# A MoE layer's gate factor in its third matrices, its residual in the experts' sum, and its last norm's sums on ScalarE

## The chip, the cores and the metric

The kernel runs on one core of a Trainium2 chip. The metric is the device time of one execution, in microseconds. The core's engines are TensorE (PE, with its weight loads apart as PEld), VectorE (DVE), ScalarE (ACT), GpSimd (POOL) and SyncE (SP, which here only starts transfers). Each engine runs its own instructions in order, and waits for the others through semaphores.

## What is computed

One decoder layer over 2048 tokens of 1024 features: a token mixer with its norm, then a mixture of experts with 64 routed experts (eight for each token) and one shared expert of 256 hidden features each. The edit touches the second half alone. Cut to that, the reference is:

```python
def layer_norm(x, g, b):
    xf = x.astype(jnp.float32)
    mu = xf.mean(-1, keepdims=True)
    var = jnp.square(xf - mu).mean(-1, keepdims=True)
    return ((xf - mu) * lax.rsqrt(var + LN_EPS)).astype(x.dtype) * g + b

def swiglu(t, w1, w3, w2):
    return (jax.nn.silu(t @ w1) * (t @ w3)) @ w2

x = layer_norm(ALPHA * x + g1 * (mixed @ w_out[l]), ln_mix_g[l], ln_mix_b[l])
h = x * (1 + sc2) + sh2
y = moe_ffn(h, ...)     # sum over a token's 8 experts of gate * swiglu, plus the shared swiglu
x = layer_norm(ALPHA * x + g2 * y, ln_ffn_g[l], ln_ffn_b[l])
```

`g2` is a vector of 1024 factors, one for each output feature, the same for all tokens. The third matrix `w2` of an expert has the output features as its columns.

## The kernel before

The first 2075 us are the mixer, its projection, its norm and the router (`phase_c` writes `ALPHA * x1`, the scaled result of the first norm, to a DRAM tensor `x1` at L1792). Then `moe_phase` (L1953 on) works through a list of units. A unit is up to 320 tokens of one set of weights. First come three units of the shared expert, 256 tokens each (set "s"), then the 64 experts, a large one and a small one in turn, each cut into one to three units, then the other 10 blocks of 128 tokens of the shared expert (set None, with its weights loaded a second time). A token block has 128 tokens.

For each set, `weights` (L1986) loads the three matrices in six halves of 512 KB: SP issues the load into one of four `wraw` buffers (L1994), ScalarE copies it to a rounded matrix (L1998), and VectorE subtracts the two for a second, small matrix (L1999), since each product runs as three matmuls of such parts. Only for the set None is the last matrix multiplied by `g2b`, a copy of `g2` on all partitions, before that (L1997). `hidden` (L2019) makes the first two products (L2051, or L2032 for at most 128 tokens), the silu on ScalarE and the product `s` on VectorE (L2057, L2038), and splits it into `gH` (ScalarE, L61) and `gL` (VectorE, L64). `transposed` does the same for the input (`hH`, `hL`) from PSUM banks named `tr`. `back` (L2060) multiplies `gH` and `gL` with the third matrix into two PSUM banks `py`. A unit's `back` is woven into the `hidden` of the unit that follows.

What happens to `py` depends on the set. `routed` scales it by the token's gate on ScalarE (L2102), and GpSimd adds it with an indirect transfer into rows of the DRAM tensor `acc` (L2103). `begin` (L2302, shared set, first six blocks) copies it on ScalarE (L2306) and writes it to `acc`; other rows of `acc` were set to zero earlier (L1567). `finish` (L2286, other ten blocks) ends the layer. It calls `sums` (L2276), which loads a block of `x1` (L2279) and, behind the last scatter-add, of `acc` (L2281), multiplies `acc` by `g2b` (L2282) and adds the two (L2283); it adds `py` to that (L2297), and starts `norm` (L2257): two statistics (L2262), their aggregate (L2264), the variance plus epsilon (L2266), a reciprocal root in ten small operations on one column (L650 to L655), two products (L2272, L2273) and the store (L2274). The six blocks that `begin` had taken need only `sums` and `norm`; one of them joins each of the first six blocks of `finish`.

The blocks under way take turns (`norms`), and a scheduler places every instruction in its engine's queue by priorities and by its own estimate of times. `y` of `finish` is one of eight buffers cut out of the weight pool (`buffer`).

## Time and profile before

| | us |
| --- | --- |
| median of three runs | 3769.25 (3760.10 to 3776.89) |
| the profiled execution | 3762.49 |
| its span on the core | 3760.8 |
| TensorE busy in the span | 3433.5 (91%) |
| VectorE busy | 2670.9 (71%) |
| ScalarE busy | 1941.9 (52%) |
| GpSimd busy | 883.3 (23%) |

The span is the time from the first to the last instruction of the profiled execution; 1.7 us lie around it. Shares are over the whole span, and hide that the stages have different limits. Times in the trace are counted from the span's start. A row of groups gives the line, the engine, the operation, the tiles written and read with their shapes, the count, the busy time and the mean of one, and the idle time of the engine just before. `<-` in brackets names what ended a wait.

### The profile page before, as it was taken

The page shows a single profiled execution, that of the slowest core. Times are in us where ns is not written, and L with a number is a line of the kernel's source. Part 1 is how long each engine was busy: PE and PEld are TensorE (multiplying, and loading weights), DVE is VectorE, ACT ScalarE, POOL GpSimd, SP SyncE. Part 2 cuts the span into 40 slices and gives each one's busy share as a digit, 9 for nine tenths or more (in the row PEclk, how much of TensorE's full clock was granted, in tenths as well). Part 3 has the DMA queues.
Part 4 walks back from the last instruction along what each step waited for, and adds up shares of the span by engine and source line. Part 5 has one row for each costly group of instructions (what it writes and reads, how often), then busy time and mean ns, then how long its engine had stood idle before and what let it go on. Part 6 is the DMA issues. An engine that isn't in the chain of part 4 may idle for free. (4 is left out here: it accounts for less than half of the span.)

```text
span 3760.8 us, 64004 instructions
## 1 busy us (share of the span) xinstructions
PE 3433.5 (91%) x23044; PEld 2984.6 (79%) x23044; DVE 2670.9 (71%) x7039; ACT 1941.9 (52%) x3439; POOL 883.3 (23%) x817
## 2 busy tenths in 40 slices
PE   7799999799999878999897899999999999999994
PEld 5577777688888767778786799888899888888983
DVE  6556899888888678888799555555665555665669
ACT  4233656355555567766322355555565555556630
POOL 1000000322223255543000122233233223232200
PEclk9899999899999889999998899999999999999997
DMA  7657466400000132222543488888899888888973
GB/s 253 210 192 242 141 216 221 164 27 21 24 24 18 30 107 81 78 69 80 172 149 129 163 213 218 234 237 233 246 266 252 242 223 235 241 248 254 295 226 138
DMA packets 276234, 640.37 MB, mean 170 GB/s; under 512 B 34428, under 2 KB 115364, under 8 KB 275784
## 3 DMA queue, kind: packets, MB, share of 16 engines
q1 hardware_dynamic: 231760, 481.09, 38.1%
q0 software_dynamic: 40832, 150.32, 18.1%
q10 hardware_dynamic: 3320, 4.83, 0.4%
q8 instruction: 182, 2.98, 0.3%
q14 instruction: 140, 1.15, 0.1%
HBM read 467.14 MB, written 169.00 MB: 169 GB/s over the span
## 5 line engine op out<-in xcount | busy, mean ns | idle before, releaser
L2051 PE MATMUL p<-hH,w 128*128 128x256 f32 (+8 forms) x4352 | 872.2, 288 | 9.3 <-DVE w L1999 6.6
L2051 PEld LDWEIGHTS p<-hH,w 128*128 128x128 f32 x4352 | 706.0, 191 | 18.8 <-DVE w L1999 6.9
L1999 DVE TENSOR_TENSOR w<-wraw,w 128x1024 fp32r<-128x1024 f32 x396 | 474.8, 1223 | 285.7 <-ACT w L1998 268.9
L2051 PE MATMUL p<-hL,w 128*128 128x256 f32 (+8 forms) x2176 | 615.9, 283 | 0.7 <-DVE hL L64 0.7
L1998 ACT ACTIVATE w<-wraw 128x1024 fp32r<-128x1024 f32 x396 | 406.1, 1053 | 232.0 <-DMA wraw<-in_exp_w_dram 102.0
L2066 PE MATMUL py<-w,gH 128*128 128x512 f32 (+5 forms) x1384 | 443.8, 403 | 26.2 <-DVE w L2297 14.6
L2103 POOL DMA_INDIRECT scratch_acc<-y,idx x157 | 263.9, 1681 | 797.5 <-ACT y L2102 245.8
L2051 PEld LDWEIGHTS p<-hL,w 128*128 128x128 f32 x2176 | 415.9, 191 | 6.2 <-DVE hL L64 0.9
L285 PE MATMUL pj<-hTH,w 128*128 128x512 f32 x1152 | 379.1, 404 | 21.5 <-ACT w L201 16.4
L64 DVE TENSOR_TENSOR hL<-tr,hH 128x512 fp32r<-128x512 f32 (+7 forms) x346 | 213.0, 626 | 210.9 <-ACT hH L61 192.7
L2066 PEld LDWEIGHTS py<-w,gH 128*128 128x128 f32 (+5 forms) x1384 | 240.5, 182 | 86.7 <-DVE w L2297 15.8
L2102 ACT ACTIVATE y<-py,gt 128x512 f32<-128x512 f32 (+5 forms) x314 | 213.9, 683 | 147.3 <-PE py L2066 131.3
L285 PEld LDWEIGHTS pj<-hTH,w 128*128 128x128 f32 x1152 | 221.9, 194 | 76.0 <-ACT w L201 20.4
L61 ACT ACTIVATE hH<-tr 128x512 fp32r<-128x512 f32 (+7 forms) x346 | 184.0, 544 | 189.6 <-PE tr L2011 165.4
L2066 PE MATMUL py<-w,gL 128*128 128x512 f32 (+5 forms) x692 | 275.9, 399 | 0.3 <-DVE gL L64 0.3
L2077 POOL DMA_INDIRECT x<-scratch_h,idx x157 | 163.5, 1041 | 309.9 <-DVE L L2119 68.5
L285 PE MATMUL pj<-hTL,w 128*128 128x512 f32 x576 | 231.2, 401 | 0.0
L2011 PE MATMUL tr<-ident,x 128*128 128x128 f32 (+5 forms) x1384 | 192.2, 266 | 31.5 <-issue 20.7
L2011 PEld LDWEIGHTS tr<-ident,x 128*128 128x128 f32 (+5 forms) x1384 | 149.8, 141 | 42.7 <-issue 26.0
L2066 PEld LDWEIGHTS py<-w,gL 128*128 128x128 f32 (+5 forms) x692 | 125.2, 181 | 40.0 <-DVE gL L64 1.7
L2032 PE MATMUL p<-w,hH 128*128 128x256 f32 (+2 forms) x736 | 142.6, 291 | 10.7 <-DVE s L2057 10.7
L61 ACT ACTIVATE gH<-s 128x256 fp32r<-128x256 f32 (+8 forms) x136 | 55.1, 405 | 160.4 <-DVE s L2057 147.8
(610 smaller groups left out, 8199.9 us busy)
## 6 DMA issues: line engine op xcount, KB each, us to landing
wraw<-in_exp_w_dram SPq DMA_DIRECT2D x384, 512.0 KB
w<-scratch_wH SPq DMA_DIRECT2D x57, 512.0 KB
w<-scratch_wL SPq DMA_DIRECT2D x57, 512.0 KB
mw<-in_w_mod_dram SPq DMA_DIRECT2D x48, 512.0 KB
scratch_rw<-po SPq DMA_DIRECT2D x44, 256.0 KB
w<-in_w_in_dram SPq DMA_DIRECT2D x21, 512.0 KB
x<-in_x_dram SPq DMA_DIRECT2D x40, 256.0 KB
scratch_wH<-w SPq DMA_DIRECT2D x19, 512.0 KB
```

The source lines that it names most:

```text
L61: nc.scalar.activation(hi, src, AF.Copy)
L64: (lo_eng or nc.vector).tensor_tensor(lo, src, hi.bitcast(F32), op=ALU.subtract)
L285: nc.tensor.matmul(ps, lhsT=a_[:, k, :], rhs=b_[k], start=(k == 0 and i == 0), stop=(k == KT - 1 and i == 2))
L1998: ACT.activation(wh[:, c], raw, AF.Copy)
L1999: V.tensor_tensor(wl[:, c], raw, wh[:, c].bitcast(F32), op=ALU.subtract)
L2011: PE.transpose(ps[:, k * n:(k + 1) * n], x[0:n, (4 * h + k) * P:(4 * h + k + 1) * P], g.ident[0:n, 0:n])
L2032: PE.matmul(ps[i][:n, 0:256], lhsT=(hH, hL)[a][:, k, 0:n], rhs=w[i][b][:, k, :], start=(k == 0 and j == 0), stop=(k == KT - 1 and j == 2))
L2051: PE.matmul(ps[i][:, 0:n], lhsT=w[i][a][:, k, m * P:(m + 1) * P], rhs=(hH, hL)[b][:, k, 0:n], start=(k == 0 and j == 0), stop=(k == KT - 1 ...
L2066: PE.matmul(ps[:n], lhsT=(gH, gL)[a][:, m, c:c + n], rhs=w[2][b][:, m, h * CH:(h + 1) * CH], start=(m == 0 and j == 0), stop=(m == 1 and j ...
L2077: G.indirect_dma_start(out=x[0:m, :], out_offset=None, in_=S["h2"], in_offset=bass.IndirectOffsetOnAxis(ap=ix[0:m], axis=0))
L2102: ACT.activation(y[:m, hs], ps[:m], AF.Copy, scale=gt[:m])
L2103: G.indirect_dma_start(out=S["acc"], out_offset=bass.IndirectOffsetOnAxis(ap=ix[0:m], axis=0), in_=y[0:m, :], in_offset=None, compute_op=A ...
```

## The change

Three edits hang together. `weights` multiplies the third matrix of every set by `g2b`, so `acc` collects sums that are already scaled. `phase_c` writes `ALPHA * x1` into `acc` itself, `begin` loads it, adds the shared expert's part on VectorE and writes it back, and the routed scatter-adds go on top: at the end `acc` holds all of the norm's input but the shared expert's last part. And the norm takes its row sum from the instruction that makes the row (an accumulator output, L2308; for the six blocks of `begin` two copies on ScalarE, L2301), its mean from those (L2264), and its variance from a square on ScalarE with the negative mean as bias and an accumulator output (L2266).

```diff
@@ phase_c
-            nc.sync.dma_start(S["x1"][t0:t0 + P, :], xh)
+            nc.sync.dma_start(S["acc"][t0:t0 + P, :], xh)
@@ weights
-                    if scaled and s is srcs[-1]:
+                    if a == 2:
                         V.tensor_tensor(raw, raw, g2b, op=ALU.mult)
@@ norm
-            for n in range(2):
-                V.bn_stats(out=st[:, n, :], in_=y[:, n * CH:(n + 1) * CH])
-            mv = sm.tile([P, 2], F32, name="lnmv")
-            V.bn_aggr(out=mv, in_=st)
-            va = sm.tile([P, 1], F32, name="lnva")
-            V.tensor_scalar(va, mv[:, 1:2], 1e-5, None, op0=ALU.add)
-            rs = rsqrt(nc, sm, va, [P, 1], None, "ln")
+            for i, (rows, y, su) in enumerate(blocks):
+                V.tensor_scalar(mean[:, i:i + 1], su[:, 0:1], su[:, 1:2], -1.0 / D, op0=ALU.add, op1=ALU.mult)
+                junk = xg.tile([P, HC], F32, name="x")[:, 0:D]
+                ACT.activation(junk, y, AF.Square, bias=mean[:, i:i + 1], accum_out=sq[:, i:i + 1])
+            yield
+            va = sm.tile([P, 2], F32, name="lnva")[:, 0:n]
+            V.tensor_scalar(va, sq, 1.0 / D, 1e-5, op0=ALU.mult, op1=ALU.add)
+            rs = rsqrt(nc, sm, va, [P, n], None, f"ln{n}")
@@ sums
-            nc.sync.dma_start(y, S["x1"][rows, :])
-            a = xg.tile([P, HC], F32, name="x")[:, 0:D]
-            nc.sync.dma_start(a, S["acc"][rows, :])
-            V.tensor_tensor(a, a, g2b, op=ALU.mult)
-            V.tensor_tensor(y, y, a, op=ALU.add)
-            return y
+            nc.sync.dma_start(y, S["acc"][rows, :])
+            return y, sm.tile([P, 2], F32, name="lnsu", bufs=8)
@@ finish
+                    for q in range(2):
+                        hs = slice(q * CH, (q + 1) * CH)
+                        junk = xg.tile([P, HC], F32, name="x")[:, hs]
+                        ACT.activation(junk, y2[:, hs], AF.Copy, accum_out=su2[:, q:q + 1])
...
-                    V.tensor_tensor(y[:, hs], ps, y[:, hs], op=ALU.add)
+                    V.scalar_tensor_tensor(y[:, hs], ps, 1.0, y[:, hs], op0=ALU.mult, op1=ALU.add, accum_out=su[:, q:q + 1])
@@ begin
+                nc.sync.dma_start(y, S["acc"][rows, :])
                 for q, ps in back(w, g_[0], g_[1], c, P):
-                    ACT.activation(y[:, q * CH:(q + 1) * CH], ps, AF.Copy)
+                    hs = slice(q * CH, (q + 1) * CH)
+                    V.tensor_tensor(y[:, hs], ps, y[:, hs], op=ALU.add)
```

VectorE's queue in the routed stage, at a pair of experts whose larger one has a unit of 288 tokens (four pairs read alike), before (-) and now (+):

```order
 L2119 TENSOR_SCALAR L<-pl,st 128x384
 L64 TENSOR_TENSOR hL<-tr,hH 128x4x128
-L2093 SCALAR_TENSOR_TENSOR jk,gt<-io,perm,x 128x64
-L2057 TENSOR_TENSOR s<-s,p_42392 128x288
+L1997 TENSOR_TENSOR wraw<-wraw,g2b 128x1024
+L2093 SCALAR_TENSOR_TENSOR jk,gt<-io,perm,x 128x64
+L1997 TENSOR_TENSOR wraw<-wraw,g2b 128x1024
+L2057 TENSOR_TENSOR s<-s,p_42494 128x288
 L64 TENSOR_TENSOR hL<-tr,hH 128x4x96
 L64 TENSOR_TENSOR gL<-s,gH 128x288
```

The two products stand ahead of the unit's `s`; the conversions of the same matrix (L1999) stay where they were, further on.

VectorE's queue near the end of the program, where the last blocks are summed and normed, before:

```order
L2282 TENSOR_TENSOR x<-x,g2b 128x1024 [waits DMAHW1_49]
L651 TENSOR_SCALAR lny<-lni 128x1 [waits DVE_49]
L64 TENSOR_TENSOR gL<-tr,gH 128x2x128 [waits Activation_49]
L653 SCALAR_TENSOR_TENSOR lna<-lny 128x1 [waits DVE_49]
L2283 TENSOR_TENSOR w<-w,x 128x1024 [waits DMAHW0_49]
L654 TENSOR_TENSOR lna<-lna,lnva 128x1 [waits DVE_49]
L2272 SCALAR_TENSOR_TENSOR w<-w,lnmv,wraw 128x1024
L655 SCALAR_TENSOR_TENSOR lny<-lna,lny 128x1 [waits DVE_49]
L2262 BN_STATS lnst<-w 128x6
```

A block's load is multiplied and added, and its statistics follow on the same engine. And now, at the same place:

```order
L2308 SCALAR_TENSOR_TENSOR w,lnsu<-py,w 128x512 [waits DMAHW1_49,PE_49]
L2277 SCALAR_TENSOR_TENSOR w<-w,ln1y,wraw 128x1024 [waits DVE_49]
L2269 TENSOR_SCALAR lnva<-lnsq 128x1 [waits Activation_49]
L2308 SCALAR_TENSOR_TENSOR w,lnsu<-py,w 128x512 [waits PE_49]
L650 TENSOR_SCALAR ln1i<-lnva 128x1 [waits DVE_49]
L64 TENSOR_TENSOR gL<-tr,gH 128x2x128 [waits Activation_49]
L651 TENSOR_SCALAR ln1y<-ln1i 128x1 [waits DVE_49]
L2264 TENSOR_SCALAR lnmean<-lnsu 128x1
L653 SCALAR_TENSOR_TENSOR ln1a<-ln1y 128x1 [waits DVE_49]
L2276 SCALAR_TENSOR_TENSOR w<-w,lnmean,wraw 128x1024
L654 TENSOR_TENSOR ln1a<-ln1a,lnva 128x1 [waits DVE_49]
L2308 SCALAR_TENSOR_TENSOR w,lnsu<-py,w 128x512 [waits DMAHW6_49,PE_49]
```

The full-width products with g2, the sums and the statistics are gone; a variance (L2269) that waits for ScalarE stands ahead of sums that read `py` (L2308).

ScalarE's queue near the end, before:

```order
L61 ACTIVATE hH<-tr 128x4x128 [waits PE_49]
L61 ACTIVATE gH<-s 128x256 [waits DVE_49]
L2056 ACTIVATE s<-p_48204 128x256 [waits DVE_49,PE_49]
L61 ACTIVATE hH<-tr 128x4x128 [waits PE_49] x2
L61 ACTIVATE gH<-s 128x256 [waits DVE_49] x2
L2037 ACTIVATE s<-p_48261 128x256 [waits DVE_49,PE_49]
L2037 ACTIVATE s<-p_48475 128x256 [waits DVE_49,PE_49]
```

It holds the splits and the silu of the last units. And now:

```order
L2301 ACTIVATE x,lnsu<-w 128x512 [waits Activation_49]
L2266 ACTIVATE x,lnsq<-w,lnmean 128x1024 [waits DVE_49]
L61 ACTIVATE gH<-s 128x256 [waits DVE_49]
L2056 ACTIVATE s<-p_48364 128x256 [waits PE_49]
L2266 ACTIVATE x,lnsq<-w,lnmean 128x1024 [waits DMAHW5_49,DMAHW6_49,DMASW5_49,DVE_49]
L61 ACTIVATE gH<-s 128x256 [waits DVE_49]
L61 ACTIVATE hH<-tr 128x4x128 [waits PE_49]
L2037 ACTIVATE s<-p_48421 128x256 [waits PE_49,Activation_49]
L61 ACTIVATE hH<-tr 128x4x128 [waits PE_49]
L2266 ACTIVATE x,lnsq<-w,lnmean 128x1024 [waits DMAHW2_49,DVE_49]
```

Squares stand between those, each behind a mean that VectorE makes.

## Rows read from the trace of the kernel before

**Rows 1.** Windows: us, busy (count) of PE, PEld, DVE, ACT, POOL, clock, DMA share

```profile
2075.00:2137.00 62.00, 51.22 (x365) 48.62 (x365) 32.76 (x82) 22.23 (x37) 4.65 (x5) 0.90 0.41 139
2137.00:3606.00 1469.00, 1431.08 (x10296) 1310.43 (x10295) 847.78 (x1912) 834.64 (x1306) 420.34 (x308) 1.00 0.87 243
...
3624.00:3761.00 137.00, 79.90 (x464) 70.08 (x462) 132.41 (x352) 10.73 (x24) 0.00 (x0) 0.80 0.46 160
```

**Rows 2.** Groups of DVE, 3624 to 3761: busy us, mean ns, idle

```profile
L2262 DVE BATCH_NORM_STATS2 lnst<-w 128x6 f32<-128x512 f32 x32 | 21.3, 672 | 0.0
L2272 DVE SCALAR_TENSOR_TENSOR w<-w,lnmv,wraw 128x1024 f32<-128x1024 f32 (+1 forms) x17 | 20.5, 1205 | 0.0
L2273 DVE SCALAR_TENSOR_TENSOR w<-w,lny,wraw 128x1024 f32<-128x1024 f32 (+1 forms) x17 | 20.4, 1206 | 0.0
L2282 DVE TENSOR_TENSOR x<-x,g2b 128x1024 f32<-128x1024 f32 x16 | 19.3, 1208 | 7.4 <-DMA x<-scratch_acc 7.4
L2283 DVE TENSOR_TENSOR w<-w,x 128x1024 f32<-128x1024 f32 x16 | 19.2, 1202 | 0.0
L2297 DVE TENSOR_TENSOR w<-py,w 128x512 f32<-128x512 f32 x20 | 13.4, 670 | 0.5 <-PE py L2066 0.5
L654 DVE TENSOR_TENSOR lna<-lna,lnva 128x1 f32<-128x1 f32 x48 | 7.0, 145 | 0.0
...
L2264 DVE BATCH_NORM_AGGREGATE lnmv<-lnst 128x2 f32<-128x12 f32 x16 | 3.1, 195 | 0.0
```

**Rows 3.** Timeline around the last stage's begin and end: start, duration

```profile
3614.70 1.55 POOL L2103 DMA_INDIRECT scratch_acc<-y,idx  x1 [6.32 <-ACT hH L61]
...
3621.08 1.27 SPq L2281 DMA_DIRECT2D x<-scratch_acc  x3
...
3624.28 1.23 DVE L2282 TENSOR_TENSOR x<-x,g2b 128x1024 f32<-128x1024 f32 x1 [7.36 <-DMA x<-scratch_acc]
...
3755.93 1.41 DVE L2273 SCALAR_TENSOR_TENSOR w<-w,lny,wraw 128x512 f32<-128x512 f32 x2
```

**Rows 4.** Groups of ACT, whole span: busy us, mean ns

```profile
L1943 ACT ACTIVATE r<-r,lnnb,lny 128x1024 f32<-128x1024 f32 x16 | 19.9, 1242 | 41.0 <-DVE lnnb L1940 41.0
L1396 ACT ACTIVATION_READ_ACCUMULATOR L<-L,mx 128x1 f32 x96 | 18.5, 193 | 0.0
...
L2306 ACT ACTIVATE y<-py 128x512 f32<-128x512 f32 x12 | 7.1, 596 | 7.7 <-PE py L2066 6.7 <-issue 0.9
```

**Rows 5.** Groups of DVE, start stage and whole span

```profile
L1685 DVE SCALAR_TENSOR_TENSOR k_oh<-k_prev,k_num,k_oh 128x64 f32<-128x64 f32 x2 | 0.5, 272 | 0.0
...
L2093 DVE SCALAR_TENSOR_TENSOR jk<-io,perm,x 128x64 f32<-128x64 f32 (+7 forms) x157 | 43.1, 275 | 0.0
...
L2093 DVE DVE_READ_ACCUMULATOR jk<-io,perm,x 128x1 f32 (+7 forms) x157 | 12.7, 81 | 0.0
```

**Rows 6.** Waits of PE and ACT, 2137 to 3606: us, times, longest

```profile
PE tr L2011 <- issue: 20.7, 11, 3.2
...
PE py L2066 <- DVE gL L64: 0.3, 1, 0.3
...
ACT w L1998 <- DMA wraw<-in_exp_w_dram: 99.9, 65, 5.8
```

**Rows 7.** Timeline of one routed expert on SP, DVE and PE

```profile
3274.06 4.47 SPq L1994 DMA_DIRECT2D wraw<-in_exp_w_dram  x3
...
3280.30 0.08 DVE L2093 DVE_READ_ACCUMULATOR jk<-io,perm,x 128x1 f32 x1
3282.24 0.46 DVE L2057 TENSOR_TENSOR s<-s,p 128x288 f32<-128x288 f32 x1 [1.86 <-issue]
...
3283.57 0.45 DVE L64 TENSOR_TENSOR gL<-s,gH 128x288 fp32r<-128x288 f32 x1
...
3298.09 0.39 PE L2066 MATMUL py<-w,gL 128*128 128x512 f32 x1
```

**Rows 8.** Timeline of DVE ahead of the shared expert's last units

```profile
3585.52 2.50 DVE L1997 TENSOR_TENSOR wraw<-wraw,g2b 128x1024 f32<-128x1024 f32 x2 [3.26 <-DMA wraw<-in_sh_w_dram]
```

More of the change, by code (lines that the diff above doesn't have):

```diff
@@ L1984, in moe_phase, with weights @@
         w2_ = lambda a: a.rearrange("(m p) n -> p m n", p=P)
-        def weights(srcs, into=None, scaled=False):
+        def weights(srcs, into=None):
             res = []
@@ L2229, in matrices @@
             if len(got) < n:
-                more_, la = weights(src[len(got):n], scaled=r is None)
+                more_, la = weights(src[len(got):n])
                 got += more_
@@ L2255, in norms, with norm @@
                 norms(True)
[L2257 to L2274 removed]
+        def norm(blocks):
+            n = len(blocks)
+            mean = sm.tile([P, 2], F32, name="lnmean")[:, 0:n]
+            sq = sm.tile([P, 2], F32, name="lnsq")[:, 0:n]
+            for i, (rows, y, su) in enumerate(blocks):
+                V.tensor_scalar(mean[:, i:i + 1], su[:, 0:1], su[:, 1:2], -1.0 / D, op0=ALU.add, op1=ALU.mult)
+                junk = xg.tile([P, HC], F32, name="x")[:, 0:D]
+                ACT.activation(junk, y, AF.Square, bias=mean[:, i:i + 1], accum_out=sq[:, i:i + 1])
+            yield
+            va = sm.tile([P, 2], F32, name="lnva")[:, 0:n]
+            V.tensor_scalar(va, sq, 1.0 / D, 1e-5, op0=ALU.mult, op1=ALU.add)
+            rs = rsqrt(nc, sm, va, [P, n], None, f"ln{n}")
+            yield
+            for i, (rows, y, su) in enumerate(blocks):
+                parts = 2 if rows.stop == T else 1
+                for q in range(parts):
+                    hs = slice(q * D // parts, (q + 1) * D // parts)
+                    V.scalar_tensor_tensor(y[:, hs], y[:, hs], mean[:, i:i + 1], ln[0][:, hs], op0=ALU.add, op1=ALU.mult)
+                    V.scalar_tensor_tensor(y[:, hs], y[:, hs], rs[:, i:i + 1], ln[1][:, hs], op0=ALU.mult, op1=ALU.add)
+                    nc.sync.dma_start(out[rows, hs], y[:, hs])
+                yield
@@ L2295, in finish @@
+                if early:
+                    under_way.append(norm(early))
+                    next(under_way[-1])
                 for q, ps in back(w, g_[0], g_[1], c, P):
                     hs = slice(q * CH, (q + 1) * CH)
-                    V.tensor_tensor(y[:, hs], ps, y[:, hs], op=ALU.add)
-                under_way.append(norm(rows, y))
+                    V.scalar_tensor_tensor(y[:, hs], ps, 1.0, y[:, hs], op0=ALU.mult, op1=ALU.add, accum_out=su[:, q:q + 1])
+                under_way.append(norm([(rows, y, su)]))
@@ L2376 @@
            ("sw", (512, T), F32), ("rw", (1408, T), F32), ("mixT", (D, T), F32), ("modrow", (8, CH), F32),
-           ("acc", (ROWS, D), F32), ("x1", (T, D), F32), ("h2", (ROWS, HC), F32), ("cum", (NE, T // 16, 18), F16), ("ovf", (NOVF, 2), F32)]
+           ("acc", (ROWS, D), F32), ("h2", (ROWS, HC), F32), ("cum", (NE, T // 16, 18), F16), ("ovf", (NOVF, 2), F32)]
 def layer(tc, A, S, out):
```

18 lines of the change are left out of this document (7 added, 11 removed).

## The prediction

> **What bounds the kernel now.** Read the windows first [rows 1]: they cut the part of the program that the edit reaches into three. In the start stage (2075 to 2137 us) and the routed stage (2137 to 3606) TensorE is the bound; in the routed stage it is busy 1431.08 of 1469 us at a granted clock of 1.00, with VectorE at 847.78 and ScalarE at 834.64 beside it. In the last stage (3624 to 3761) the picture turns over: VectorE is busy 132.41 of 137 us, TensorE 79.90 at a mean clock of 0.80, ScalarE 10.73. The timeline shows why it begins there [rows 3]: the last scatter-add is issued at 3614.70, the loads of `acc` follow at 3621.08, VectorE has been idle for 7.36 us when it starts at 3624.28, and from there it hardly stops until its last product ends at 3757.34 (3755.93 + 1.41). The groups show what it does there [rows 2]: the only idle time ahead of any group is the 7.4 us at the start and 0.5 us before L2297. So the last stage is a queue on VectorE 133.1 us long, and each microsecond taken out of that queue shortens the kernel until the next engine is as late.
>
> **The change in the last stage.** Removed from VectorE: 16 products with g2 (L2282, 19.3), 16 sums (L2283, 19.2), 32 statistics (L2262, 21.3) and 16 aggregates (L2264, 3.1), 62.9 us in 80 instructions [rows 2]. These durations overlap a little: all groups of the stage add to 157.8 us (the eight shown to 124.2, ten smaller ones to 33.6) against 132.41 us of merged busy time [rows 1] in 352 instructions, so each hides 0.072 us under the next. The 80 removed ones occupy 62.9 - 80 x 0.072 = 57.1 us.
>
> Added to VectorE: 16 one-column means, like the small operations of L654 (145 ns, 0.07 net), 1.1 us; and 20 accumulator reads, since the sum with PSUM (L2308 in place of L2297) now also gives row sums. The trace has that pair: an accumulator read is 81 ns, and the 128x64 three-operand instruction takes 275 ns with an accumulator (L2093) and 272 without (L1685) [rows 5]. So the main instruction stays at L2297's 670 ns [rows 2], and the reads cost 20 x 0.08 = 1.6 us. The queue is then 133.1 - 57.1 + 2.7 = 78.7 us.
>
> A rule of the Trainium skill speaks against this step: Vector Engine (DVE) Microarchitecture Reference, section 7, says that an instruction of this shape with two non-bf16 SBUF sources runs at half throughput because nothing is left for the accumulator. L2273, of that shape with two fp32 SBUF sources and no accumulator, takes 1206 ns, a plain product of that size 1208 [rows 2], so the trace does not agree without an accumulator; with one, over 512 columns, no row of before shows it. By the rule the 20 sums would cost another 20 x 0.53 = 10.7 us, and the kernel would gain 22 us instead of 33.
>
> Added to ScalarE: 16 squares of 128x1024 with a bias and an accumulator, and 12 copies of 128x512 with one. The nearest rows are L1943 (1242 ns) and L2306 (596 ns), with 193 ns for an accumulator read [rows 4]: 16 x 1.44 + 12 x 0.79 = 32.4 us on top of 10.73, 43 us. ScalarE has the room. TensorE's remaining work is 79.90 us at 0.80, about 64 at full clock.
>
> So VectorE stays the longest, but its queue is no longer self-sufficient. Each block's mean now goes to ScalarE for the square and comes back for the variance, and VectorE's instructions are in order: behind a variance that waits stand the PSUM sums, which free `py` for TensorE. The price of one round trip is a square with its read, 1.44 us. If every trip of 16 is covered by other blocks' work, the cost is 0; if none is, 23 us. I take the middle, 12 us, since the new order puts 2 to 12 instructions between a block's mean and its variance in the first blocks and none in the last one. Last stage: -57.1 + 2.7 + 12 = **-42 us, from -54 to -31**. The loads of `acc` don't change their start: they still wait for the last scatter, and the 512 KB loads of x1 that stood ahead of them are gone.
>
> **The change in the routed stage.** 130 new products of 128x1024 on VectorE, two for each of 64 experts and two for the shared expert's first load. The row is L1997, which exists before for the last weights alone: two in 2.50 us, behind 3.26 us of waiting for the load [rows 8]. 130 x 1.25 = 163 us, of which some 157 fall in the routed stage's 1469 us; VectorE goes from 847.78 to about 1005 us there, still far under TensorE. Nothing of that is on the path by itself. What matters is where it stands. In VectorE's order the pair sits ahead of the next `s` product, and it waits for the landing of w2 itself, where before VectorE took w2 only after ScalarE's conversion, much later. One expert shows the size [rows 7]: VectorE is free at 3280.38, and SP issues three loads in 3274.06 to 3278.53, the last two of them w2. Where ScalarE waited for a weight (65 times [rows 6]) the load had landed 3.9 to 10.8 us after its issue began, 6.2 at the median; I walk with 5.2. The last load, begun at 3278.2, lands at about 3283.4, the product behind it ends at 3284.7, and the `s` product of 3282.24 starts there, 2.5 us late. The same walk over the 50 sets of weights that I could place gives from nothing to 6.0 us, mostly 2.5 to 4.8.
>
> What waits for the late instructions? `s` gives `gL`, and that `gL` of 3283.57 is multiplied on TensorE at 3298.09, 14 us later [rows 7], since the units are interleaved. Over all units (159 `gL` and 346 `hL` paired with their first use in program order) a quarter of the `gL` has under 3.0 us of room and a quarter of the `hL` under 7.5; in the walk the lateness exceeds the room in two sets, by 0.3 us in sum. TensorE's waits agree that VectorE's results are rarely last: 0.3 us on `gL` in the whole stage [rows 6]. What is left is TensorE's own idle time, 1469 - 1431 = 38 us [rows 1], of which 20.7 us stands ahead of the transposes at L2011 [rows 6], whose banks VectorE frees. With 18.5% more in VectorE's queue (157 of 848) I lengthen those 38 us by as much, **+7 us**; bounds 0 (the walk) and 32 (half a microsecond in each of 64 experts). ScalarE's part is the same instructions as before, and the product adds nothing to the chain of w2, since ScalarE comes to it later than VectorE.
>
> **Start stage.** VectorE takes 12 sums of 670 ns (L2320) from ScalarE's 12 copies of 596 (L2306) [rows 2, 4], 4 products more, and waits for 6 loads of `acc` that did not exist. TensorE is idle 62 - 51.22 = 11 us there, and VectorE, 32.76 of 62 busy [rows 1], has room for 8 + 5 us. I take **+2**, from 0 to 5. The store of x1 into `acc` instead of a tensor of its own is the same number of stores of the same size: 0.
>
> **Sum.** -42 + 7 + 2 = -33. The profiled execution took 3762.49 us (span 3760.8), so it would take about 3729; the median of the runs shown is 3769.25, 6.8 us above it, and the forecast goes against that: **3736 us**.
>
> **Rivals.** (A) The waits between VectorE and ScalarE take the place of the work removed: every square bare (23 us), and TensorE, held at `py`, keeps the low clock of the stage, 80 us instead of 64 (16 us). The last stage gains 57 - 3 - 39 = 15 us, with 9 lost elsewhere: about 3763. For it: one in-order queue now holds the PSUM sums behind ScalarE, and ScalarE's copies wait for loads ahead of `hH`, which TensorE needs. Against it: eight buffers for the blocks, and several blocks under way at once.
> (B) Slower: the product at w2's landing stalls the routed stage. At w2's load VectorE stands; with a longer landing (ScalarE's waits for weights show up to 5.8 us beyond its arrival [rows 6]) the lateness passes the rooms above, and TensorE loses it once per expert. At 1 us for 64 experts: -42 + 64 + 2, 3793 us. It decides from (42 - 2) / 64 = 0.6 us per expert; from 0.9 us the kernel is slower by over 0.5%. Against it: the rooms of 3 to 14 us.
> (C) The halved accumulating sum of the skill's section 7: 3769.25 - 22 = 3747. That rule rests on its page alone; the row of 275 against 272 ns speaks against it.
>
> **How the numbers follow.** Forecast 0.63, A 0.20, B 0.12, C 0.05. The range holds the forecast with its bounds (-54 to -31 in the last stage, 0 to 37 before it: 3715 to 3775), A and C: **3715 to 3775**; B is left out. 0.5% is 19 us, about what a measurement of this kernel tells from no change. Faster: forecast and C, 0.68; same: A, 0.20; slower: B, 0.12.
>
> **What would show it.** In the profile after, the last stage from VectorE's first sum to the end lasts 91 + 3.5 us instead of 133.1 + 3.5; L2308 lasts 670 ns (1200 by C); VectorE's idle time there stands ahead of L2269, the variance, behind ACT L2266, and is 5 to 20 us. The routed stage (the first routed transposes to the last) is 1469 + 7 us, with waits `<-DMA wraw` ahead of L1997 of 150 us or more in all that no TensorE row names. I would be wrong if TensorE's waits on VectorE grew by over 30 us, or if ScalarE's L2301 held `hH` behind a load for 2 us a block.

## The result and the profile after

The changed kernel takes **3802.74 us** (median of 6 runs, 3790.91 to 3810.64) against 3773.07 for the kernel before, measured beside it: ratio 1.0071, interval 1.0046 to 1.0096. One of the six runs of the kernel before was slow (4804.35 us) and is left out of the ratio. The forecast was 3736, faster by 1%, in a range up to 3775; the kernel is slower by 0.7% and the time lies above the range.

The profiled execution (3809.17 us, span 3807.5, against 3762.49 and 3760.8) shows where. Four marks cut both traces: TensorE's first product of the expert part (2074.30 before, 2082.74 after), the first scatter-add of an expert's rows (2162.77 and 2174.43), the last one (3614.70 [rows 3] and 3709.60), and the end.

| stretch | before, us | after, us | difference | forecast |
|---|---|---|---|---|
| ahead of the expert part | 2074.3 | 2082.7 | +8.4 | 0 |
| start stage, to the first scatter-add | 88.5 | 91.7 | +3.2 | +2 |
| routed stage, first to last scatter-add | 1451.9 | 1535.2 | **+83.3** | +7 |
| last stage, last scatter-add to the end | 146.1 | 97.9 | **-48.2** | -42 |

The first row holds the same code in both kernels but for the name of a stored tensor; it is a difference from run to run and no effect. The two profiled executions lie 46.7 us apart, where the ratio says 27, so some 20 us of the differences in this table come from which executions were profiled. The last stage kept what was forecast and more. The routed stage took all of it back, and it is what the experiments are about.

The windows of the routed stage, before and then after (columns as in [rows 1]: length, busy time and count of PE, PEld, DVE, ACT, POOL, granted clock, DMA share, GB/s):

```profile
2162.77:3614.70 1451.93, 1414.01 (x10170) 1294.39 (x10169) 837.50 (x1885) 825.11 (x1291) 418.14 (x305) 1.00 0.87 243
```

```profile
2174.43:3709.60 1535.17, 1447.12 (x10116) 1309.39 (x10115) 975.49 (x2006) 819.71 (x1288) 431.97 (x305) 0.98 0.83 228
```

VectorE is 138 us busier, as intended, and has 560 us to spare. TensorE was idle 37.9 us and is now idle 88.1: +50. And the same products keep it busy 33 us longer, at a granted clock of 0.98 instead of 1.00. Both parts make up the +83: 1.3 us for each of 64 experts on the mean.

TensorE's waits in that stretch, before:

```profile
PE tr L2011 <- issue: 20.7, 11, 3.2
...
PE tr L2011 <- DVE cj L2139: 4.3, 5, 1.8
...
PE p L2051 <- DVE hL L64: 0.7, 1, 0.7
```

and after:

```profile
PE tr L2011 <- issue: 34.9, 11, 4.9
PE p L2051 <- DVE hL L64: 13.5, 16, 1.5
PE tr L2011 <- DVE gL L64: 8.1, 4, 4.2
...
PE tr L2042 <- DVE s L2038: 5.4, 5, 2.2
PE py L2066 <- ACT gH L61: 4.6, 3, 2.7
```

No single line carries the 50 us. By the whole list the time is spread over results of VectorE (14 us before, 40.8 after), of ScalarE (1.2 and 12.2) and over stalls for which the profile names no releaser (20.7 and 34.9). So the waits behind them have to be read. ScalarE's wait for `s`, before (2137 to 3606):

```profile
ACT gH L61 <- DVE s L2057: 95.5, 61, 4.9
```

The waits of VectorE and ScalarE for the routed experts' weights and of ScalarE for `s`, after (2145 to 3700):

```profile
ACT gH L61 <- DVE s L2057: 205.6, 88, 9.8
...
ACT w L1998 <- DMA wraw<-in_exp_w_dram: 135.6, 60, 7.0
DVE wraw L1997 <- DMA wraw<-in_exp_w_dram: 118.2, 67, 6.3
```

ScalarE's wait for a late `s` was 95.5 us before and is 205.6; that for raw weights was 99.9 [rows 6] and is 135.6; the product's own wait is new. The chain of work that ended last says it in one line each, before and after:

```profile
PE 35%; DVE 4%; DMA 2%; issue 1%; ACT 1%; SPq 0%; DVEq 0%; POOLq 0%; ACTq 0%
```

```profile
PE 28%; DMA 6%; DVE 5%; issue 2%; ACT 2%; DVEq 0%; ACTq 0%; SPq 0%; POOLq 0%
```

Transfers (DMA) went from 2% of the span to 6% of it on that chain; loads of the routed experts' raw weights are 2% before and 5% after. The shares add to 43%, the part of the span that the chain covers.

One place shows how it happens (timeline of the routed stage, after; start, duration):

```profile
3404.30 1.23 DVE L1997 TENSOR_TENSOR wraw<-wraw,g2b 128x1024 f32<-128x1024 f32 x1 [0.36 <-DMA wraw<-in_exp_w_dram]
...
3405.92 0.45 ACT L61 ACTIVATE gH<-s 128x288 fp32r<-128x288 f32 x1 [3.65 <-DVE s L2057]
...
3406.64 1.99 ACT L1998 ACTIVATE w<-wraw 128x1024 fp32r<-128x1024 f32 x2
...
3408.98 10.74 SPq L1994 DMA_DIRECT2D wraw<-in_exp_w_dram  x6
...
3417.04 1.06 ACT L1998 ACTIVATE w<-wraw 128x1024 fp32r<-128x1024 f32 x1 [1.38 <-DMA wraw<-in_exp_w_dram]
...
3418.13 1.22 DVE L1999 TENSOR_TENSOR w<-wraw,w 128x1024 fp32r<-128x1024 f32 x1 [1.17 <-ACT w L1998]
...
3419.27 0.23 DVE L2139 TENSOR_SCALAR_CACHE_REDUCE cj<-tr,pos 128x16 f32<-128x16 f32 x1
...
3419.80 1.09 PE L2011 MATMUL tr<-ident,x 128*128 128x128 f32 x4 [4.86 <-issue]
...
3420.54 1.20 PE L2066 MATMUL py<-w,gH 128*128 128x512 f32 x2
```

The product stands ahead of `s`, which VectorE makes at 3405.44; ScalarE has stood 3.65 us for it, and behind it in ScalarE's queue stand two conversions of raw weights (3406.64), whose subtractions on VectorE free the raw buffers, for which SP's next six loads (3408.98) wait. The next expert's conversions then wait for their loads (2.30 us at 3414.27, 1.38 at 3417.04), VectorE's subtraction for the conversion, the token count of L2139, which reads a `tr` bank, stands behind that subtraction, and TensorE begins its transposes 0.3 us after it, 4.86 us idle (L2140, the last to read that bank, ends at 3419.70, 0.1 us before them). That the bank was TensorE's releaser is read from these times; the profile names none. And the matmul pair behind the stall takes 1.20 us, where one of that form takes 0.62 at the full clock (at 3298.32 before). The windows around it give the clock:

```profile
3404.00:3414.00 10.00, 10.00 (x75) 9.12 (x73) 8.67 (x16) 6.06 (x9) 3.66 (x3) 1.00 0.71 180
3414.00:3419.80 5.80, 0.94 (x9) 0.79 (x8) 3.20 (x7) 3.67 (x6) 1.10 (x1) 0.93 1.04 299
3419.80:3426.00 6.20, 6.20 (x18) 5.05 (x19) 4.60 (x11) 1.28 (x2) 1.00 (x1) 0.51 0.77 264
3426.00:3436.00 10.00, 10.00 (x77) 9.18 (x77) 2.39 (x7) 4.25 (x8) 3.63 (x4) 1.00 0.55 115
```

After 5.8 us with 0.94 us of work, the granted clock is 0.51, the 1.2 GHz level, for 6.2 us, and then 1.00 again. This stall is paid for twice.

The last stage, its groups of VectorE (3719 to 3808, columns as in [rows 2]):

```profile
L2308 DVE SCALAR_TENSOR_TENSOR w<-py,w 128x512 f32<-128x512 f32 x20 | 13.7, 687 | 3.0 <-PE py L2066 2.9
...
L2264 DVE TENSOR_SCALAR lnmean<-lnsu 128x1 f32<-128x1 f32 x16 | 3.4, 210 | 2.2 <-ACT x L2301 2.1
...
L2269 DVE TENSOR_SCALAR lnva<-lnsq 128x1 f32<-128x1 f32 x16 | 2.3, 150 | 1.8 <-ACT x L2266 1.8
...
L2308 DVE DVE_READ_ACCUMULATOR w<-py,w 128x1 f32 x20 | 1.7, 85 | 0.0
```

and its window:

```profile
3719.00:3808.00 89.00, 73.45 (x502) 66.07 (x500) 80.45 (x308) 37.00 (x81) 0.00 (x0) 0.96 0.53 194
```

VectorE still sets this stage, 80.45 of 89 us against 132.41 of 137 [rows 1]. The four groups L2282, L2283, L2262 and the old L2264 [rows 2] are gone, and VectorE waits 1.8 us for squares (L2269) and 2.1 us for the sums of ScalarE's copies (L2264).

### The profile page after: what moved, and what is told of

Same layout as the page of the kernel before. It is cut to its first block, busy times and chain, and to the rows that moved or that the text cites. A ratio compares the mean times of both kernels' runs of the same rounds, so it can differ in the third digit from the quotient of the medians.

```text
span 3807.5 us, 64077 instructions
## 1 busy us (share of the span) xinstructions
PE 3470.5 (91%) x23044; PEld 3005.2 (79%) x23044; DVE 2774.6 (73%) x7137; ACT 1957.3 (51%) x3483; POOL 896.8 (24%) x817
## 5 line engine op out<-in xcount | busy, mean ns | idle before, releaser
L1999 DVE TENSOR_TENSOR w<-wraw,w 128x1024 fp32r<-128x1024 f32 x396 | 474.5, 1223 | 236.3 <-ACT w L1998 232.8
L2066 PE MATMUL py<-w,gH 128*128 128x512 f32 (+5 forms) x1384 | 454.8, 411 | 9.4 <-ACT gH L61 5.7
L2102 ACT ACTIVATE y<-py,gt 128x512 f32<-128x512 f32 (+5 forms) x314 | 213.3, 684 | 144.6 <-PE py L2066 143.0
L1997 DVE TENSOR_TENSOR wraw<-wraw,g2b 128x1024 f32<-128x1024 f32 x132 | 161.0, 1225 | 130.7 <-DMA wraw<-in_exp_w_dram 118.2
L2011 PE MATMUL tr<-ident,x 128*128 128x128 f32 (+5 forms) x1384 | 198.0, 271 | 49.2 <-issue 34.9
L2011 PEld LDWEIGHTS tr<-ident,x 128*128 128x128 f32 (+5 forms) x1384 | 153.5, 143 | 60.3 <-issue 37.9
```

What stands on the lines that cost most here:

```text
L1997: V.tensor_tensor(raw, raw, g2b, op=ALU.mult)
L1999: V.tensor_tensor(wl[:, c], raw, wh[:, c].bitcast(F32), op=ALU.subtract)
L2011: PE.transpose(ps[:, k * n:(k + 1) * n], x[0:n, (4 * h + k) * P:(4 * h + k + 1) * P], g.ident[0:n, 0:n])
L2066: PE.matmul(ps[:n], lhsT=(gH, gL)[a][:, m, c:c + n], rhs=w[2][b][:, m, h * CH:(h + 1) * CH], start=(m == 0 and j == 0), stop=(m == 1 and j ...
L2102: ACT.activation(y[:m, hs], ps[:m], AF.Copy, scale=gt[:m])
```

## The experiments

All times below are ratios to the kernel before, measured beside it, with 95% intervals; "routed" and "last" are the two stretches of the table above, from each kernel's profile. A profile is one execution, and executions of one kernel lie up to 28 us apart (held, 3766.76 to 3794.66), so where it matters a cost is given by the ratios too.

### Which part costs, which gains

**norm_only**: the new norm on ScalarE alone. The routed weights, x1's own tensor, `begin` and the products with g2 at the end are as before.

```diff
-                    if a == 2:
+                    if scaled and s is srcs[-1]:
...
-            nc.sync.dma_start(y, S["acc"][rows, :])
+            nc.sync.dma_start(y, S["x1"][rows, :])
+            a = xg.tile([P, HC], F32, name="x")[:, 0:D]
+            nc.sync.dma_start(a, S["acc"][rows, :])
+            V.tensor_tensor(a, a, g2b, op=ALU.mult)
+            V.tensor_tensor(y, y, a, op=ALU.add)
```

> Only the norm's part of the change: row sums from the accumulator, squares on ScalarE; weights, x1, begin and the two full-width instructions on acc are those of before. Theory W (the product's wait for w2 holds VectorE and, behind it, ScalarE and TensorE) and theory V (the 130 products are simply too much work for VectorE in the routed stage) both put the loss in the routed stage, so here it keeps its length within 5 us, and the last stage loses the statistics: 21.3 + 3.1 us less 48 overlaps of 0.07 is 21 us off VectorE's queue, 2.7 us come back: about 18 us faster than before, ratio 0.995. If the norm on ScalarE were itself what costs (theory N: round trips that hold TensorE), it would be no faster than before.

Ratio 0.9961 (0.9941 to 0.998); last stage 134.5 us, so 11.6 of the 48 us. The other 36.6 go with the full-width products and sums, which took 38.5 us of VectorE (L2282, L2283 [rows 2]).

**no_product**: the changed kernel with g2 in the shared expert's third matrix only.

```diff
-                    if a == 2:
+                    if scaled and a == 2:
...
-                more_, la = weights(src[len(got):n])
+                more_, la = weights(src[len(got):n], scaled=r in (None, "s"))
```

> The whole change, but the routed experts' third matrices are left without g2 (the shared expert's keep it), so the routed part of the sum is not scaled. Theories W and V: the routed stage returns to its length of before and the last stage keeps its gain of 48 us, so about 3722 us, ratio 0.987. Theory B (what costs is the residual in acc, its loads in begin, and the sums there, which shift the start of the routed stage): still 3800, ratio 1.007.

Ratio 0.9877 (0.9841 to 0.9912), routed 1461.1, last 97.8:

```profile
2168.03:3629.14 1461.11, 1419.09 (x10132) 1292.88 (x10131) 836.92 (x1882) 825.87 (x1289) 421.01 (x305) 0.99 0.86 239
```

The last stage keeps its gain, and 74 of the 83 us of the routed stage are gone with 128 products; by the ratios these cost 73 us. The other 9 us are not explained by them; norm_only, whose routed code is that of before, shows 1456.8, so some 5 us of it lie within what runs differ by.

### Is it the wait or the work?

**wait_only**: the product stands where it stood and waits for the same load, but touches 8 of 1024 columns in the routed experts.

```diff
-                        V.tensor_tensor(raw, raw, g2b, op=ALU.mult)
+                        m_ = slice(0, 1024 if scaled else 8)
+                        V.tensor_tensor(raw[:, m_], raw[:, m_], g2b[:, m_], op=ALU.mult)
```

> As the change, but the product with the routed experts' third matrices takes 8 of 1024 columns, so the rest of the features is not scaled: VectorE stands at the same place of its queue until the same load has landed, but then works 0.15 us instead of 1.23. Theory W: most of the loss stays, 3780 to 3800 us, ratio 1.002 to 1.008, and ScalarE's idle time ahead of gH behind the s product stays near 200 us in the routed stage. Theory V: nearly all of it goes, 3722 to 3732 us, ratio 0.987 to 0.990, and that idle time returns to about 95 us.

Ratio 0.9948 (0.9929 to 0.9968), routed 1483.3: 22 us above no_product (27 by the ratios), about a third of the loss, which neither theory had. VectorE waits longer for the loads than in the changed kernel (116 us in that stretch), and ScalarE nearly as long for `s` (200.6 there):

```profile
DVE wraw L1998 <- DMA wraw<-in_exp_w_dram: 189.7, 114, 5.5
ACT gH L61 <- DVE s L2058: 174.2, 88, 7.3
```

So waits of an engine, however long in sum, don't price the loss.

**work_only**: the 2 x 1.22 us of work without a new wait. After the subtraction of w3's halves VectorE multiplies a spare tile of its own; the experts' w2 is not scaled, so g2 is missing in the routed output.

```diff
                     V.tensor_tensor(wl[:, c], raw, wh[:, c].bitcast(F32), op=ALU.subtract)
+                    if not scaled and a != 2 and len(srcs) - len(res) == 2:
+                        V.tensor_tensor(spare, wl[:, c].bitcast(F32), g2b, op=ALU.mult)
```

> As the kernel without the routed products, with two products of 128x1024 added for each routed expert that read a tile VectorE itself has just written (the small matrix of w3, ahead or between the conversions) and write a tile that nobody reads; routed third matrices stay without g2. So VectorE gets the work of the change, 157 us in the routed stage, but no new wait. If the work in itself costs (theory V), the loss of the narrow wait, 24 us, and this one add up to the 76 of the change: 3727 + 52 = 3780 us, ratio 1.003. If work and wait only hurt together because they stand between the hL and the s of a unit (theory W, widened: a held stretch of VectorE costs what it exceeds the room behind it), this stays below the 28 us of the late products: 3728 to 3750 us, ratio 0.988 to 0.994.

Ratio 0.9984 (0.997 to 0.9999), routed 1507.9: 47 us above no_product (40 by the ratios). The median, 3772.21 us, lies above theory W's range and short of V's 3780. TensorE's waits have moved to VectorE's results:

```profile
PE tr L2014 <- DVE tk L2143: 15.3, 5, 3.9
PE tr L2014 <- DVE hL L64: 15.3, 5, 3.8
PE tr L2014 <- DVE gL L64: 13.8, 5, 4.8
```

Wait (22) and work (47) add up to nearly the 74. But the work stands at another place of the queue here, so this is no clean split.

**at_gate**: more work on VectorE, at another place. w2 stays unscaled; VectorE applies gate and g2 together to the expert's output, where before ScalarE applied the gate (L2102).

```diff
-                ACT.activation(y[:m, hs], ps[:m], AF.Copy, scale=gt[:m])
+                V.scalar_tensor_tensor(y[:m, hs], ps[:m], gt[:m], g2b[:m, hs], op0=ALU.mult, op1=ALU.mult)
```

> g2 is applied where a routed block leaves PSUM: one instruction on VectorE, (py x gate) x g2b, in place of ScalarE's scaled copy; the routed third matrices stay as they are, the shared expert's carry g2, and the last stage is the change's. VectorE gets 312 instructions of some 0.7 us, 218 us, more than the 157 of the products, but no wait for a load: it waits for TensorE's py, which ScalarE waited for until now. Theory V (work costs): at or above the change, 3800 us or more. Theory W: it costs only what py is late, 3735 to 3765 us, ratio 0.990 to 0.998.

Ratio 0.9938 (0.992 to 0.9957), routed 1471.5, 10 us above no_product. That profile is the shortest of nine executions (3736.85 us, median 3754.00); by the ratios the cost is 23 us:

```profile
2166.65:3638.10 1471.45, 1420.91 (x10141) 1293.33 (x10141) 1045.66 (x2194) 630.36 (x977) 416.39 (x305) 0.99 0.86 237
```

VectorE is busier than in any kernel so far, 1045.66 us, 70 more than in the changed one, and the stage is 64 us shorter. So the amount of work on VectorE alone doesn't set the loss. What the kernel gains here by taking 190 us from ScalarE is part of that cost, and isn't separated.

**late_product**: product, conversion and subtraction of w2 are issued a unit later, and the product behind the first `s` of the unit under way.

```diff
+                    def split(a=a, raw=raw, wh=wh, wl=wl, c=c):
+                        if a == 2:
+                            with tc.issue_after(mark[0]) if mark[0] is not None and later is not None else ExitStack():
+                                V.tensor_tensor(raw, raw, g2b, op=ALU.mult)
...
+                first = V.tensor_tensor(s[:, 0:n], s[:, 0:n], ps[1][:, 0:n], op=ALU.mult).ins
+                mark[0] = first if m == 0 else mark[0]
```

> The whole change with the same products of full width, each pair placed in VectorE's queue behind the first s product of the unit under way instead of ahead of it; loads, conversions and everything else as in the change. Theory W: the load has mostly landed when VectorE comes to it, s and gH are no longer late, and the kernel gains most of the last stage's 48 us: 3725 to 3750 us, ratio 0.988 to 0.995. Theory V: the work is the same, so 3790 to 3805 us, ratio 1.005 to 1.009.

Ratio 0.9963 (0.9943 to 0.9983), routed 1486.4: 49 us less than the change, 25 more than no_product (32 by the ratios), a little slower than theory W's range. ScalarE's wait for `s` is back near the 96.5 us of before in that stretch, and the product hardly waits; ScalarE's wait for raw weights stays at 117.9 (98.7 before):

```profile
ACT gH L61 <- DVE s L2065: 87.4, 51, 3.0
...
DVE wraw L2001 <- DMA wraw<-in_exp_w_dram: 19.9, 13, 3.4
```

### Another engine

**on_pool**: the routed products on GpSimd.

```diff
-                        V.tensor_tensor(raw, raw, g2b, op=ALU.mult)
+                        (V if scaled else G).tensor_tensor(raw, raw, g2b, op=ALU.mult)
```

> The whole change with the routed products on GpSimd instead of VectorE (the shared expert's stay on VectorE). VectorE's queue in the routed stage is that of before. Theory W and V: the loss on VectorE goes; GpSimd, 420 us busy in 1452, gets 128 products of perhaps 2 to 3 us and waits for w2 ahead of gathers and scatters. If those have room, 3727 to 3745 us, ratio 0.988 to 0.993; if the gathers come late (each waits for the one queue), TensorE waits ahead of its transposes and it is at or above 3770.

Ratio 1.0215 (1.018 to 1.025), routed 1581.9. The second half of the expectation came, a time above 3770. A product takes twice as long there and stands among the gathers and scatters:

```profile
L1997 POOL TENSOR_TENSOR wraw<-wraw,g2b 128x1024 f32<-128x1024 f32 x128 | 321.6, 2535 | 87.7 <-DMA wraw<-in_exp_w_dram 77.2 <-issue 3.5 <-ACT hH L61 3.5
```

And it lengthens VectorE's own instructions. Without the 128 products VectorE is busy 836.92 us in no_product and 1002.98 here, more than in the changed kernel, which makes them itself. The subtractions, in no_product and then here:

```profile
L1999 DVE TENSOR_TENSOR w<-wraw,w 128x1024 fp32r<-128x1024 f32 x380 | 455.5, 1222 | 276.0 <-ACT w L1998 274.5 <-PE tr L2011 0.5
```

```profile
L1999 DVE TENSOR_TENSOR w<-wraw,w 128x1024 fp32r<-128x1024 f32 x380 | 517.2, 1384 | 290.3 <-ACT w L1998 288.7
```

The 63 of them that run beside a product of GpSimd's take 2.20 us on the mean, the other 317 take 1.22. So it is with others that read two tiles in SBUF (the gate of L2093, 2.30 us against 0.28). Those that read PSUM are as fast beside a product: 0.69 us for the `hL` of 128x512 either way. How much of the loss comes from this and how much from late gathers isn't separated.

**norm_pool**: norm_only, with the last stage's full-width product and sum on GpSimd.

```diff
-            V.tensor_tensor(a, a, g2b, op=ALU.mult)
-            V.tensor_tensor(y, y, a, op=ALU.add)
+            G.tensor_tensor(a, a, g2b, op=ALU.mult)
+            G.tensor_tensor(y, y, a, op=ALU.add)
```

> No product in the weights at all: x1 and acc apart as before, the norm on ScalarE as in the change, and the last stage's two full-width instructions per block (acc x g2b, plus x1) on GpSimd, which is idle there. VectorE's queue in the last stage is then that of the change, about 80 us, if GpSimd keeps up: 32 instructions of 128x1024 in 90 us leave it 2.8 us each. If one takes 1.2 to 2.5 us: gain of 40 to 48 us, 3722 to 3732, ratio 0.987 to 0.990. If it takes 4 us, GpSimd is the bound with 128 us and the gain is that of the norm alone or less, 3755 or more. The routed stage is as before in each case.

Ratio 1.0092 (1.0068 to 1.0117), last stage 175.4 us instead of 134.5, where 1.2 to 2.5 us for an instruction was to gain 40 us or more. GpSimd's queue doesn't fill the stage: its products of 2.7 us and sums of 2.4 keep it busy 83.5 us, and it waits 67.7 us for loads of `acc`. VectorE is busy 131.8 us, where the changed kernel's queue takes 80.45, since here too its instructions stretch beside GpSimd's. A one-column product of the reciprocal root took 145 ns [rows 2] and now takes up to 2.33 us:

```profile
L654 DVE TENSOR_TENSOR ln1a<-ln1a,lnva 128x1 f32<-128x1 f32 x48 | 20.3, 425 | 0.4
```

### The place in the queue, or the loop through the raw buffers?

A raw buffer is loaded by SP, multiplied (w2), converted by ScalarE, subtracted by VectorE, and only then free for the next load. Four buffers carry that loop. The product lengthens it (loop), and it delays whatever stands behind it on VectorE (place). A fifth buffer loosens the loop.

```diff
-        wr = right("e_wr", 4)
+        wr = right("e_wr", 5)
```

**after_wr5** and **before_wr5** are the two kernels with that line alone.

> The changed kernel with five wraw buffers instead of four, nothing else. Theory L (a held VectorE comes late to L1999, frees the buffers late, and the loads of the next set start late): a fifth buffer takes much of that away, at least 30 of the 76 us that the routed products cost: 3740 to 3772 us, ratio 0.992 to 1.000. Theory P (what VectorE delivers late is PSUM banks and s, straight to TensorE and ScalarE; loads are not on that path): 3795 to 3805, ratio 1.006 to 1.009, like the change.

> The kernel before with five wraw buffers, as the control: what the fifth buffer is worth where no product stands in the way. TensorE's idle time in the routed stage is 38 us in all, 21 of it ahead of the transposes. Theory L: 0 to 15 us faster, less than the changed kernel gains by it: ratio 0.996 to 1.000. Theory P: no change, ratio 1.000 within its interval.

Both came outside both theories. The control gained: before_wr5 0.9909 (0.9877 to 0.994). after_wr5 lost: 1.0169 (1.0126 to 1.0211), routed 1566.2. With a buffer more, the loads are issued earlier, and the scheduler put the products earlier in VectorE's queue too, some ahead of the token lists (L2140 to L2145) that the gathers need. The waits show it:

```profile
ACT gH L61 <- DVE s L2057: 240.9, 89, 13.0
DVE wraw L1997 <- DMA wraw<-in_exp_w_dram: 196.5, 68, 11.8
...
POOL x L2077 <- DVE hL L64: 94.7, 24, 13.1
```

This run alone could not tell place from loop, since both had changed. **at_gate_wr5** and **late_wr5** are those two kernels with the fifth buffer.

> g2 applied at the gate on VectorE, with five wraw buffers. The routed stage of the version with four is 10 us longer than that without routed products. Theory L: these 10 us and some of before's idle time go, 3725 to 3745 us, ratio 0.987 to 0.993. Theory P: as with four buffers, ratio 0.994.

> The late products with five wraw buffers. With four, the routed stage is 25 us longer than without routed products. Theory L: half or more of that goes, 3730 to 3745 us, ratio 0.988 to 0.993. Theory P: as with four buffers, 3756 us, ratio 0.996.

Ratios 0.9816 (0.9774 to 0.9858) and 0.9812 (0.9771 to 0.9853): the best versions with g2 in the whole output, some 70 us under the kernel before and 35 under before_wr5, and below the ranges of both theories.

**held**, **held_wr5** and **no_product_wr5** close the gap. In held the products are written as in late_product, but told to stand behind the newest token list instead of behind `s`, which puts them about where the change had them, mostly 1 to 8 instructions ahead of the next `s` (2 at the median, 5 in the change). held_wr5 is that with the fifth buffer; the last is no_product with it. The diff is against late_product.

```diff
-                first = V.tensor_tensor(s[:, 0:n], s[:, 0:n], ps[1][:, 0:n], op=ALU.mult).ins
-                mark[0] = first if m == 0 else mark[0]
+                V.tensor_tensor(s[:, 0:n], s[:, 0:n], ps[1][:, 0:n], op=ALU.mult)
...
-            V.tensor_tensor(idx[:, 0:n], tk[:, 0:n], pd[:, 0:n], op=ALU.add)
+            mark[0] = V.tensor_tensor(idx[:, 0:n], tk[:, 0:n], pd[:, 0:n], op=ALU.add).ins
```

> The changed kernel, its products told to stand behind the newest token list (the idx sum) of VectorE, four buffers as before: VectorE's order is then nearly that of the changed kernel, a product 1 to 8 rows ahead of the next s. A control of the rewriting. If place decides: like the changed kernel, 3790 to 3810 us, routed stage 1520 to 1540. If the way of ordering them gains by itself: below 3775.

> The same places with five buffers for the raw weights. Theory loop (the loss comes from the loop load, product, conversion, subtraction, free buffer, which one more buffer loosens whatever the place): as the late product gained, 50 us, 3740 to 3755. Theory place (VectorE standing at w2 ahead of s is the loss; a buffer doesn't help there): 3785 to 3810, and VectorE's wait for raw weights at the product grows over 118 us.

> The changed kernel without g2 in the routed experts (that product is left out of the output), five buffers: the floor under the late product and the gate with five buffers. The kernel before gained 36 us from the fifth buffer, so 3727 - 36 = 3691; if the late product at 3701 hides wholly, 3695 to 3705; if it still costs its 28 us, 3665 to 3680.

| product | 4 buffers | routed, us | 5 buffers | routed, us |
|---|---|---|---|---|
| none in routed experts | 0.9877 | 1461.1 | 0.9772 (0.9738 to 0.9806) | 1419.8 |
| held behind the token list | 1.0021 (1.0 to 1.0043) | 1521.4 | 0.9852 (0.9825 to 0.988) | 1453.3 |
| late, behind `s` | 0.9963 | 1486.4 | 0.9812 | 1432.5 |
| with the gate | 0.9938 | 1471.5 | 0.9816 | 1431.7 |
| the change | 1.0071 | 1535.2 | 1.0169 | 1566.2 |

Read the routed columns down for place: with four buffers the held product costs 60 us over none, the late one 25, the gate 10; with five, 34, 13 and 12. Read across for the loop: where the place stays, the fifth buffer gives 41 us without products and 68 with the held ones. So about half of the held product's cost, 27 of 60 us, goes with a buffer and is the loop; 34 us stay, and moving the product behind `s` takes 21 of them.

By the ratios the costs over none are 54, 32 and 23 us with four buffers and 30, 15 and 17 with five, and the loop's share of the held product is 24 of 54; each ratio is known to 7 to 16 us. Held above late and gate with four buffers is clear of that; the order of late and gate is not, and the share of the loop and the 15 to 21 us of place with five buffers are sizes only roughly known. The place isn't quite the same either: with the fifth buffer a held product stands 4 instructions ahead of the next `s` at the median, not 2. held came just under the range for place, held_wr5 under those of both theories, and VectorE's wait at the product, which place had grow, fell from 114.2 to 83.5 us; no_product_wr5 came near its 3691 (3693.71). Both theories hold a part. What the fifth buffer does is seen in the chain of work that ended last, held, held_wr5 and no_product_wr5:

```profile
PE 28%; DMA 7%; DVE 5%; ACT 2%; issue 2%; DVEq 0%; ACTq 0%; SPq 0%
```

```profile
PE 31%; DVE 4%; DMA 4%; ACT 2%; issue 2%; DVEq 0%; ACTq 0%; SPq 0%; POOLq 0%
```

```profile
PE 39%; DVE 2%; issue 1%; DMA 0%; ACT 0%; DVEq 0%; SPq 0%; ACTq 0%; POOLq 0%
```

and ScalarE's wait for raw weights, held and held_wr5:

```profile
ACT w L2002 <- DMA wraw<-in_exp_w_dram: 120.5, 65, 7.3
```

```profile
ACT w L2002 <- DMA wraw<-in_exp_w_dram: 37.4, 17, 3.8
```

Without products too, TensorE's stalls for which the profile names no releaser belong to the loop. no_product has

```profile
PE tr L2011 <- issue: 22.7, 11, 3.5
```

and in no_product_wr5 and before_wr5 there is no such line.

held costs 0.5% less than the change in nearly the same order; the change's own places are worse by 14 us in the routed stage, and which of them make that is open. Open too is how the 34 us that stay split between ScalarE's queue behind `gH`, the transposes' banks and the gathers: no run here takes one of them away alone.

## Why the prediction was wrong

**The last stage: right.** -48 against -42, inside -54 to -31. The main term held: VectorE's queue there is shorter by the instructions removed. L2308 takes 681 ns at the median in no_product and 687 in the changed kernel, with 84 ns for the accumulator read, where 670 and 80 were taken. The term that was mis-sized is the round trips to ScalarE: 12 us taken, 1.8 + 2.1 measured, near the lower end of that bound, 0. The work of the other blocks covers nearly all of them; no run takes eight buffers or the turns of the blocks away to show which of the two does it. Rival A (trips bare, low clock) is refuted by the same rows and by a clock of 0.96 in the stage.

**Rival C** wanted 1200 ns for L2308 and is refuted. The Trainium skill's rule (Vector Engine (DVE) Microarchitecture Reference, section 7) speaks of two non-bf16 sources in SBUF; L2308 has one in PSUM, so the rule doesn't cover it and was no argument against this step. at_gate's instruction of that shape with one source in PSUM and one in SBUF, without an accumulator (L2102), takes 746 ns. With two SBUF sources and an accumulator the runs have L2093 alone, over 64 columns, and its 275 ns against 272 without show no halving; a longer row no run here has. The 1206 ns of L2273 were misread: that mean holds two instructions of half the width, and the 15 of 1024 columns take 1267 ns, 5% more than the plain product and far from double.

**The start stage: inside its range**, +3.2 against +2, which the runs don't tell from nothing: the same stretch lasts 89.9 us in norm_only, whose start stage is that of before, and 89.2 in no_product, whose is that of the change.

**The routed stage is the step that failed**: +7 forecast with a bound of 32, +83 measured. Rival B, at 0.12, had the sign, the place and nearly the price: the product at w2's landing stalls TensorE, by 1.3 us for each expert on the mean (1.15 against no_product) where it was priced at 1. It had only a part of the way there, VectorE's lateness at `gL` and `hL`; the way through ScalarE's queue and the raw buffers isn't in it. Three sentences of the step were wrong:

- "Nothing of that is on the path by itself." The walk asked only when TensorE needs `gL` and `hL`, found room for both, and left a residue of 0.3 us. It stopped one engine too early. ScalarE needs `s` for `gH` at once, and in its queue the conversions of raw weights stand behind that `gH`: its wait there went from 95.5 to 205.6 us. What share of the loss went that way isn't measured by itself. TensorE's waits on VectorE's results grew by 27 us, below the 30 that I had named as the sign of being wrong, and still the stage lost 83.
- "the product adds nothing to the chain of w2, since ScalarE comes to it later than VectorE." It adds to the loop through four raw buffers, and that loop was near the path already: before_wr5 gains 0.9% with one more buffer and no other change, and loads were 2% of the chain of before. The held pair puts the loop at some 27 us (24 by the ratios).
- The 38 us of TensorE's idle time were scaled with VectorE's busy time, 18.5%. at_gate makes VectorE busier still and costs 10 us (23 by the ratios), though ScalarE has less to do there: busy time is no measure of this. And the idle time was taken at its own length, where the clock adds to it: 50 us of idle time came with 33 us of slower work.

**The signs I had named.** The wait for raw weights ahead of L1997 was to be 150 us or more that no TensorE row names: 118.2. That was a sign of the mechanism and not of its price: wait_only waits 189.7 us and loses 22. VectorE's idle time ahead of L2269 was to be 5 to 20 us and is 1.8. ScalarE's copies (L2301) wait 5.3 us for loads in all, 5.0 of them at the stage's begin, far from 2 us a block.

## What to carry to other kernels

An instruction added to an engine with time to spare is priced by what stands behind it in that engine's queue, followed through the next engine's queue too, and by every buffer that it keeps from being free. Ask whether that loop is already near the path; one buffer more in the kernel before answers it, at the cost of one run. Where work must be added, put it behind what others wait for (here behind `s`, or with the gate), and then give the loop a buffer: that order of steps turned +0.7% into -1.9%, of which the kernel before gets 0.9% from the buffer alone. An idle engine isn't a free place: work moved to GpSimd made VectorE's own instructions longer.

## What the runs showed of the hardware

- TensorE's granted clock after a stall: 5.8 us with 0.94 us of work, then 0.51 for 6.2 us (the 1.2 GHz level), then 1.00. Over the routed stage it was 1.00 in late_wr5 (TensorE 21 us idle), 0.98 in the change (88) and 0.96 in on_pool (122):

```profile
2183.56:3765.50 1581.94, 1460.38 (x10136) 1324.95 (x10135) 1002.98 (x1883) 826.48 (x1288) 755.95 (x429) 0.96 0.81 221
```

- A 128x1024 fp32 product takes 2535 ns on GpSimd in the routed stage and 2707 ns in the last stage, against 1.22 us on VectorE (the trace's spans on GpSimd are rough):

```profile
L2287 POOL TENSOR_TENSOR x<-x,g2b 128x1024 f32<-128x1024 f32 x16 | 43.3, 2707 | 77.2 <-DMA x<-scratch_acc 67.7 <-PE p L2051 9.5
```

- Beside such a product, VectorE's instructions with two SBUF sources run long: 2.20 us on the mean for the subtraction of 128x1024 against 1.22 apart from it (on_pool), up to 2.33 us for one column against 0.16 (norm_pool). Those with a source in PSUM don't: 0.69 us for 128x512 in both cases.

- An accumulator on a VectorE sum from PSUM over 512 columns costs its read of 85 ns and 11 to 17 ns more in the instruction; on ScalarE a square of 128x1024 with bias and accumulator takes 1154 ns and its read 185 (estimates of 1242 and 193 had been taken from [rows 4]):

```profile
L2266 ACT ACTIVATE x<-w,lnmean 128x1024 f32<-128x1024 f32 x16 | 18.5, 1154 | 32.9 <-DVE lnmean L2264 17.0 <-issue 12.4 <-DVE ln1a L654 2.5
...
L2266 ACT ACTIVATION_READ_ACCUMULATOR x<-w,lnmean 128x1 f32 x16 | 3.0, 185 | 0.0
```
